# Loading the second quarter of w in eight transfers instead of four, row sets 0 and 1 of all quadrants ahead of row sets 2 and 3

## The chip, the core and the metric

The kernel runs on one core of a Trainium2 chip. The metric is the time of one launch on the device in microseconds (us); for the kernel before, the median of 8 runs is 905.83 us (905.59 to 906.26). A profiled execution gives, besides its time, the span between the first and the last instruction of its trace, and all positions below ("at 14.59") are us from the start of that span.

The core's engines are written as in the profile: PE (matrix multiply), PEld (its weight loads), DVE (vector), ACT (scalar), POOL and SP. POOL and SP also issue transfers; q0 is the queue of those that POOL issues, q1 and q10 those that SP and ACT issue.

## What is computed

```python
B, S, D = 16, 2048, 1024          # x (B,S,D), w (D,D), decay (D), all float32
xw = x @ w
out[:, 0, :] = xw[:, 0, :]
for t in range(1, S):
    out[:, t, :] = decay * out[:, t - 1, :] + xw[:, t, :]
```

A matrix product of 32768 x 1024 by 1024 x 1024, and behind it, for every column of every batch, a first-order recurrence along the 2048 time steps.

## The kernel before

**Tiling.** The 32768 rows of x are cut into 64 chunks of 512 time steps; two chunks make a group. For each group the 1024 output columns are cut into 8 blocks n of 128. One (group, n) is a tile: PE accumulates 128 columns by 1024 steps in PSUM, over K = 8 blocks k of 128 contraction rows, in bf16. Then ACT, POOL and DVE run the recurrence, DVE turns the result back, and SP stores it. There are some 4,000 matmuls of 128x512.

**x.** `load(c, q, j0, j1)` (L101) issues from POOL the transfer of quadrant q (256 of the 1024 contraction rows, on 32 partitions) of chunk c, cast to bf16 on the way. DVE turns it by blocks of 32 (`turn`, L110), and ACT or DVE spreads it into `xt` (`part`, L119). The matmuls of the first chunks read partly `xw` (straight from the turn) and partly `xt`.

**w.** w comes in four quarters (h, e): h is the half of the columns, e the parity of the rows. `stage[h, e]` holds a quarter as it lands; `settle(h, e, m, copy)` (L300) copies row set m (m = 0 to 3) of it into `wsb`, block k = 2m + e. So k = 0, 2, 4, 6 come from e = 0 and k = 1, 3, 5, 7 from e = 1. Quarter (0, 0) is loaded by SP and ACT in float32; the other three by POOL, cast to bf16. `load_w` (L293) issues one transfer for each quadrant of a quarter, in the order 0, 2, 1, 3.

**The order.** All work is emitted in an order written out by hand: `agenda` is a list of deeds, a letter and a number, and the order within one engine's queue is the order of the list. The first line (key -99) is what concerns us, with these letters:

- `M0` to `M3` (`load_half`): the four quadrant transfers of one half of chunk 0 (M0, M1) or chunk 1 (M2, M3), 128 KB each in bf16
- `U0`, `U1`, `U2` (`load_part`, L339): the quarters (0, 1), (1, 0) and (1, 1) of w
- `K0` to `K3`: matmuls that only keep PE busy, each set behind the landing of a quadrant of M0
- `E0` to `E15`: turns of one row set of half a chunk on DVE; `G` and `F`: their spreading on ACT and DVE (E0 to E3 belong to M0, E4 to E7 to M1, E8 to E11 to M2, E12 to E15 to M3)
- `W4 w5 W6 W7`: `settle` of quarter (0, 1), row sets 0 to 3, W on DVE and w on ACT; later `W8` to `W11` settle (1, 0), and `w12` to `w15` settle (1, 1)
- `L`: one more quadrant of a later chunk of x

The transfers of POOL use eight completion semaphores in turn. A transfer therefore waits, on POOL's queue, until the one eight places before it has landed; what stands behind it on that queue waits too.

**Step 0 of PE** is special. In order, for the first four blocks n at once: the even k on chunk 0's two halves (from `xw`, 128x256, 32 matmuls), the odd k on chunk 0 (from `xt`, 128x512, 16 matmuls: k = 1, 3, 5, 7, four each), then chunk 1's first half (k in pairs, 32 matmuls of 128x256), then its second half. So PE needs, in this order: M0 and M1, then row sets 0 to 3 of quarter (0, 1), then M2, then M3. Blocks n = 4 and up need the quarters (1, 0) and (1, 1).

Of the kernel before, what the change touches and what calls it, by code (L numbers as in the profile page):

```python
# [14 lines left out]
def _ap(ap_obj: bass.AP, new_ap, extra_offset=0):  # L15
    return dataclasses.replace(
        ap_obj,
        ap=[list(p) for p in new_ap],
        offset=ap_obj.offset + extra_offset,
    )  # L20
# [5 lines left out]
def kernel(  # L26
# [26 lines left out]
    nc = tc.nc  # L53
    pin = tc.keep_in_program_order
    B, S, D = x.shape
# [3 lines left out]
    P = 32  # L59
    CQ = D // NQ  # L60
    K = CQ // P
    M = K // 2
# [4 lines left out]
    CH = D // 2  # L67
# [12 lines left out]
    def quad(q):  # L80
        return slice(q * P, (q + 1) * P)
# [184 lines left out]
    class Outlet:  # L266
# [7 lines left out]
        def store(self, b, t0):  # L274
# [3 lines left out]
            for i, q in enumerate((0, 2, 1, 3)):  # L278
# [9 lines left out]
    stage = {(0, 0): room[0][:, 0:size],  # L288
             (0, 1): room[0][:, size:size * 3 // 2].bitcast(BF16),
             (1, 0): room[1][:, 0:size // 2].bitcast(BF16),  # L290
             (1, 1): room[1][:, size // 2:size].bitcast(BF16)}

    def load_w(queues, h, e):  # L293
        for i, q in enumerate((0, 2, 1, 3)):
            pin(queues[i % len(queues)].dma_start(  # L295
                out=stage[h, e][quad(q)].rearrange("p (m d) -> p m d", m=M),
                in_=_ap(w, [[2 * D, P], [2 * P * D, M], [1, CH]],
                        (q * CQ + e) * D + h * CH)))

    def settle(h, e, m, copy):  # L300
        src = stage[h, e][:, m * CH:(m + 1) * CH]
# [5 lines left out]
    rows = const.tile([128, 2, P], FP32, name="rows")  # L307
    touch = const.tile([128, 1], BF16, name="touch")
    load_w((nc.sync, nc.scalar), 0, 0)
    pin(nc.vector.memset(idle, 0.0))  # L310
    pin(nc.vector.memset(rows, 0.0))
# [13 lines left out]
    for q in range(NQ):  # L325
        pin(nc.sync.dma_start(
            out=rows[q * P:q * P + R],
            in_=_ap(decay, [[P, R], [CH, 2], [1, P]], q * CR)))
# [8 lines left out]
        spin(3 if q < NQ - 1 else 2, gates[q])  # L337

    def load_part(i):  # L339
        load_w((nc.gpsimd,), *((0, 1), (1, 0), (1, 1))[i])  # L340

    def part_one(i, copy):
        part(i // 8, copy, i % 4, i % 4 + 1, *halves[i // 4 % 2])
# [60 lines left out]
    def turn_and_load(c):  # L404
# [16 lines left out]
        "w": lambda i: settle_one(i, nc.scalar.copy),  # L421
        "M": load_half,
        "U": load_part,
        "E": lambda i: turn(i // 8, *halves[i // 4 % 2], i % 4, i % 4 + 1),
        "F": lambda i: part_one(i, nc.vector.tensor_copy),
# [15 lines left out]
        "L": lambda i: load(*loads.pop(0)) if loads else None,  # L441
    }
    agenda = {
        -99: "M0 M1 U0 M2 M3 U1 U2 w0 W1 w2 W3 K0 K1 K2 K3 E0 E1 G0 E2 G1 E3 F2 G3 E4 E5 G4 E6 G5 E7 F6 G7 W4 w5 W6 W7 D E8 E9 G8 E10 G9 E11 F10 G11 E12 L E13 G12 L E14 G13 E15 L F14 G15",
        0: "p0 z0 W8 W9 W10 W11",
        1: "g0",
        2: "L S1 L",
# [186 lines left out]
```

## Time and profile before

| | us |
|---|---|
| median of 8 runs | 905.83 |
| the profiled execution, its own time | 905.89 |
| its span | 904.1 |
| PE busy | 891.6 (99%) |
| DVE busy | 825.7 (91%) |
| ACT busy | 684.4 (76%) |
| POOL busy | 655.2 (72%) |
| PE idle before L131 matmuls | 5.2, of which 0.7 for `wsb` from DVE |

Busy is the sum of instructions, idle is the time that an engine sat still in front of a group of instructions, and the releaser is what ended it. Issuing a transfer occupies POOL (some 0.55 to 0.65 us each), and the time from issue to landing is listed for itself.

### The profile page before, as it was taken

Reading aid. Unit: us, or ns where it says so; the run is one execution under the profiler, and the core shown is the slowest. Engines: PE = TensorE matmul, PEld = TensorE weight load, DVE = VectorE, ACT = ScalarE, POOL = GpSimd, SP = SyncE. Lnnn points to the kernel's source line nnn. Section 1 sums busy time; section 2 is a strip of 40 time slices with the busy share of each in tenths; the row PEclk is TensorE's granted clock in tenths of the full one; section 3 lists DMA queues with packets and bytes.
Section 4 is the critical chain, followed back from the end, with each engine's and each line's share of the span. In section 5 each row is a group of like instructions: output and inputs, shape, how many; then the busy total and the mean of one; then the engine's idle time right before and its main releaser. Section 6 shows DMA issues by size and latency. Waiting matters only on the chain.

```text
span 904.1 us, 11988 instructions
## 1 busy us (share of the span) xinstructions
PE 891.6 (99%) x4119; PEld 411.0 (45%) x4201; DVE 825.7 (91%) x628; ACT 684.4 (76%) x951; POOL 655.2 (72%) x753
## 2 busy tenths in 40 slices
PE   8999999999999999999999999999999999999997
PEld 5544444444444444444444444444444444444444
DVE  4999998999999999999998999999999999999997
ACT  4889867777877877877778778778777787787742
POOL 7888678777767768777677677787777776776622
PEclk9999999999999999999999999999999999999999
DMA  9999999999999999999999999999999999999868
GB/s 191 197 215 215 231 238 212 215 230 251 242 240 256 250 244 260 248 249 228 225 235 231 221 232 229 228 228 230 228 227 225 234 233 223 227 235 207 175 146 229
DMA packets 402542, 204.77 MB, mean 226 GB/s; under 512 B 8752, under 2 KB 401456, under 8 KB 402480
## 3 DMA queue, kind: packets, MB, share of 16 engines
q1 hardware_dynamic: 265168, 134.76, 61.0%
q0 software_dynamic: 137024, 68.70, 56.7%
q8 instruction: 33, 0.54, 0.2%
q10 hardware_dynamic: 288, 0.52, 0.2%
q14 instruction: 29, 0.24, 0.1%
HBM read 138.42 MB, written 134.22 MB: 302 GB/s over the span
## 4 chain that ended last, share of the span: by engine, by line
PE 95%; DMA 1%; DVE 1%; issue 1%; ACT 1%; POOL 0%; DVEq 0%; POOLq 0%
PE ps L131 94%; PE spare L131 1%; DVE so L221 1%; DMA xb<-in_x_dram 1%; DMA ot<-in_w_dram 1%; ACT xs L183 0%; ACT xt L123 0%; DVE so L201 0%; POOL ot L295 0%; POOL xs L196 0%; ACT h L169 0%; DVE ot L258 0%; PE spare L383 0%; PE ps L383 0%; DVE h L387 0%
## 5 line engine op out<-in xcount | busy, mean ns | idle before, releaser
L131 PE MATMUL ps<-xt,wsb 128*128 128x512 bf16 x3942 | 863.5, 378 | 5.2 <-DVE wsb L302 0.7
L131 PEld LDWEIGHTS <-wsb 128*128 128x128 bf16 x4152 | 405.9, 98 | 480.2 <-DVE wsb L302 1.0
L196 POOL TENSOR_TENSOR xs<-h,xs 128x512 f32<-128x512 f32 (+1 forms) x189 | 241.9, 1280 | 190.0 <-ACT h L169 84.8
L183 ACT COPY xs<-ps 128x1024 f32<-128x1024 f32 (+1 forms) x189 | 188.8, 999 | 154.7 <-PE ps L131 144.3
L258 DVE STREAM_TRANSPOSE ot<-so 128x1024 f32<-128x1024 f32 (+1 forms) x260 | 300.1, 1191 | 2.1 <-POOL so L190 1.1
L246 POOL TENSOR_TENSOR so<-h,xs 128x512 f32<-128x512 f32 (+1 forms) x189 | 240.5, 1274 | 44.9 <-ACT h L169 28.2
L123 ACT COPY xt<-xw 128x2048 bf16<-128x2048 bf16 (+1 forms) x136 | 242.3, 1790 | 7.3 <-DVE xw L115 7.1
L105 POOL DMA_DIRECT2D xb<-in_x_dram x264 | 174.0, 660 | 3.0 <-DMA ot<-in_w_dram 1.2
L169 ACT ACTIVATE h<-so,dec 128x512 f32<-128x512 f32 (+1 forms) x189 | 144.9, 767 | 28.6 <-DVE so L201 25.5
L115 DVE STREAM_TRANSPOSE xw<-xb 128x2048 f32<-128x2048 f32 (+1 forms) x78 | 147.3, 1901 | 7.1 <-DMA xb<-in_x_dram 7.1
L201 DVE TENSOR_TENSOR_SCAN so<-spare,keep,xs 128x512 f32<-128x512 f32 (+1 forms) x96 | 119.3, 1244 | 26.6 <-POOL xs L196 26.2
L201 DVE TENSOR_TENSOR_SCAN so<-spare,xs 128x512 f32<-128x512 f32 x93 | 113.2, 1219 | 27.4 <-POOL xs L196 24.6
L169 ACT ACTIVATE h<-ps,dec 128x512 f32<-128x512 f32 (+1 forms) x189 | 129.7, 686 | 0.0
L221 DVE TENSOR_TENSOR_SCAN so<-dec,ps 128x1024 f32<-128x1024 f32 x34 | 76.9, 2261 | 1.3 <-ACT h L169 1.0
L221 DVE TENSOR_TENSOR_SCAN so<-dec,keep,ps 128x1024 f32<-128x1024 f32 (+1 forms) x36 | 77.2, 2145 | 0.5 <-PE ps L131 0.3
L250 ACT COPY keep<-so 128x1 f32<-128x1 f32 x136 | 25.3, 189 | 12.9 <-DVE so L221 12.6
L192 ACT COPY so<-keep 128x1 f32<-128x1 f32 x96 | 18.3, 191 | 2.0 <-DVE ot L258 1.8
L131 PE MATMUL ps<-xw,wsb 128*128 128x256 bf16 (+1 forms) x68 | 11.2, 301 | 0.0
L190 POOL MEMSET so<- 128x1 f32 x93 | 10.7, 117 | 0.3 <-DVE ot L258 0.3
L131 PE MATMUL spare<-xt,wsb 128*128 128x512 bf16 (+1 forms) x48 | 10.0, 335 | 0.0
L295 POOL DMA_DIRECT2D ot<-in_w_dram x12 | 6.5, 544 | 3.0 <-DMA xb<-in_x_dram 2.1
L320 PE MATMUL spare<-idle 128*128 128x512 bf16 x22 | 6.3, 452 | 1.2 <-DVE idle L310 1.2
(37 smaller groups left out, 36.3 us busy)
## 6 DMA issues: line engine op xcount, KB each, us to landing
out_dram<-ot SPq DMA_DIRECT2D x248, 512.0 KB, 10.9
xb<-in_x_dram POOLq DMA_DIRECT2D x248, 256.0 KB, 7.8
out_dram<-ot SPq DMA_DIRECT2D x12, 256.0 KB, 4.8
xb<-in_x_dram POOLq DMA_DIRECT2D x16, 128.0 KB, 5.8
ot<-in_w_dram POOLq DMA_DIRECT2D x12, 128.0 KB, 5.1
out_dram<-xb SPq DMA_DIRECT2D x3, 256.0 KB
ot<-in_w_dram ACTq DMA_DIRECT2D x2, 256.0 KB, 5.0
ot<-in_w_dram SPq DMA_DIRECT2D x2, 256.0 KB, 4.6
```

Of the source, the lines that this page charges most:

```text
L105: pin(nc.gpsimd.dma_start(out=xb_of[c][quad(q), j0:j1], in_=_ap(x, [[D, P], [P * D, j1 - j0], [1, CQ]], (b * S + t0 + j0 * P) * D + q * CQ)))
L115: pin(nc.vector.transpose(out=dst.rearrange("p (m j i) -> p j m i", m=M, i=P)[:, j0:j1, m0:m1], in_=src.rearrange("p (j m c) -> p j m c", ...
L123: pin(copy(out=xt_of[c][:, m0:m1, :, j0 * P:j1 * P], in_=src))
L131: pin(nc.tensor.matmul(out=ps[:, t0:t1] if ps.shape[1] >= t1 else ps, lhsT=lhs, rhs=rhs, start=(k == 0 and t0 == start), stop=(k == K - 1),))
L169: pin(nc.scalar.activation(out=h, in_=src, func=mybir.ActivationFunctionType.Copy, scale=dec[:, self.n:self.n + 1]))
L183: pin(nc.scalar.copy(out=self.xs, in_=self.ps))
L196: pin(nc.gpsimd.tensor_tensor(out=odds, in0=self.g, in1=odds, op=ALU.add))
L201: pin(nc.vector.tensor_tensor_scan(out=so[:, 3:T + 2:2], data0=squares[-1][:, n:n + 1].to_broadcast([128, T // 2]), data1=self.xs[:, 1:T:2 ...
L221: pin(nc.vector.tensor_tensor_scan(out=so[:, t + 2:t + 2 + size], data0=dec[:, n:n + 1].to_broadcast([128, size]), data1=ps, initial=befor ...
L246: pin(nc.gpsimd.tensor_tensor(out=self.so[:, 2:T + 2:2], in0=self.h, in1=self.xs[:, 0:T:2], op=ALU.add))
L250: pin(nc.scalar.copy(out=self.keep, in_=self.so[:, self.T + 1:self.T + 2]))
L258: pin(nc.vector.transpose(out=outlet.ot[:, :, c0:c0 + P], in_=self.so[:, 2 + t0:2 + t0 + nj * P].rearrange("p (i t) -> p i t", t=P)))
```

## The change

`load_w` takes two further arguments, the first and last row set that it loads, and quarter (0, 1) is loaded by two calls: row sets 0 and 1 of the four quadrants, then row sets 2 and 3. Each transfer has 64 rows of 512 elements in place of 128. The list gains one deed, the later ones are renumbered, and all the rest is as it was.

```diff
-    def load_w(queues, h, e):
+    def load_w(queues, h, e, m0=0, m1=M):
         for i, q in enumerate((0, 2, 1, 3)):
             pin(queues[i % len(queues)].dma_start(
-                out=stage[h, e][quad(q)].rearrange("p (m d) -> p m d", m=M),
-                in_=_ap(w, [[2 * D, P], [2 * P * D, M], [1, CH]],
-                        (q * CQ + e) * D + h * CH)))
+                out=stage[h, e][quad(q)].rearrange("p (m d) -> p m d", m=M)[:, m0:m1],
+                in_=_ap(w, [[2 * D, P], [2 * P * D, m1 - m0], [1, CH]],
+                        (q * CQ + e + m0 * 2 * P) * D + h * CH)))
...
     def load_part(i):
-        load_w((nc.gpsimd,), *((0, 1), (1, 0), (1, 1))[i])
+        load_w((nc.gpsimd,), *((0, 1, 0, 2), (0, 1, 2, M), (1, 0), (1, 1))[i])
...
-        -99: "M0 M1 U0 M2 M3 U1 U2 w0 W1 w2 W3 K0 K1 K2 K3 ...
+        -99: "M0 M1 U0 U1 M2 M3 U2 U3 w0 W1 w2 W3 K0 K1 K2 K3 ...
```

On POOL's queue the order becomes: eight transfers of chunk 0 (M0, M1), eight of quarter (0, 1) (64 KB each in bf16), eight of chunk 1 (M2, M3), eight of the quarters (1, 0) and (1, 1), and then chunk 2. POOL issues 4 transfers more. On DVE, `W4` waits for the first four transfers of the quarter alone, and `W6` for the other four; on ACT, `w5` needs the first four. The order of instructions on PE, DVE, ACT and SP is unchanged.

## The prediction

> **What bounds the kernel now.** First the page: PE is busy for 99% of the span, and the chain that ended last runs on it.
>
> ```profile
> span 904.1 us, 11988 instructions
> PE 891.6 (99%) x4119; PEld 411.0 (45%) x4201; DVE 825.7 (91%) x628; ACT 684.4 (76%) x951; POOL 655.2 (72%) x753
> ```
>
> So a delay of PE near the start, with PE hardly ever idle behind it, arrives at the end in full. Next, what PE waited for between 8 and 60 us:
>
> ```profile
> PE spare L320 <- ACT gate L336: 0.9, 1, 0.9
> PE ps L131 <- DVE wsb L302: 0.7, 1, 0.7
> ```
>
> The second wait (us in total, times, longest) is the only one that this change can remove. The timeline shows it, on PE and on DVE (start, duration, in brackets the idle time before):
>
> ```profile
> 14.31 0.27 PE L131 MATMUL spare<-xw,wsb 128*128 128x256 bf16 x1
> 15.29 0.82 PE L131 MATMUL ps<-xt,wsb 128*128 128x512 bf16 x2 [0.70 <-DVE wsb L302]
> ```
> ```profile
> 14.94 0.70 DVE L302 COPY wsb<-ot 128x512 bf16<-128x512 bf16 x3 [1.09 <-DMA ot<-in_w_dram]
> 17.66 1.43 DVE L115 STREAM_TRANSPOSE xw<-xb 128x256 f32<-128x256 f32 x4 [1.47 <-DMA xb<-in_x_dram]
> 20.38 0.77 DVE L115 STREAM_TRANSPOSE xw<-xb 128x256 f32<-128x256 f32 x2 [0.98 <-DMA xb<-in_x_dram]
> ```
>
> W4 starts when the four transfers of quarter (0, 1) have landed (the last at 9.74 + 5.07 = 14.81, by the chain in order of time), and PE sits still until 15.29. But the next two things on DVE, the turns of M2 (17.66) and M3 (20.38), wait for transfers as well. So I read the queue that feeds all of them, POOL's:
>
> ```profile
> 7.89 0.55 POOL L295 DMA_DIRECT2D ot<-in_w_dram  x1 [1.85 <-DMA xb<-in_x_dram]
> 8.68 1.61 POOL L295 DMA_DIRECT2D ot<-in_w_dram  x3 [0.23 <-DMA xb<-in_x_dram]
> 10.40 3.04 POOL L105 DMA_DIRECT2D xb<-in_x_dram  x5
> 13.78 1.99 POOL L105 DMA_DIRECT2D xb<-in_x_dram  x3 [0.34 <-DMA ot<-in_w_dram]
> ```
>
> The reader is to see that POOL issues no faster than landings allow: the ninth transfer goes out at 7.89, 0.29 after the first landed (1.32 + 6.28 = 7.60). Eight are in flight, and a quarter of w holds four of the eight places. Finally the rate, from 10.6 to 13.3 us:
>
> ```profile
> DMA packets 711, 0.54 MB, mean 198 GB/s; under 512 B 66, under 2 KB 711, under 8 KB 711
> ```
>
> One 128 KB transfer takes 131072 / 198 = 0.66 us of the DMA engines. Single issues, asked for one by one, landed 5.1 (M2's first, issued at 10.40) to 5.4 us after issue. Is the rest of these 5 us queueing, which shorter transfers would shorten, or fixed? A stretch in which q0 was empty tells:
>
> ```profile
> q1 hardware_dynamic: 2004, 1.01, 102.9%
> xb<-in_x_dram POOLq DMA_DIRECT2D x2, 256.0 KB, 10.3
> ```
>
> From 129.0 to 132.7 only SP's stores move; POOL's issue at 130.15 shows its first packet at 132.74, so 2.6 us from issue to first byte. At the start, an engine that had run dry took w's first packet at 10.66, 2.8 us after the issue at 7.89. I take 2.7. Before the change M2's first transfer is issued at 10.40 and ready at 13.1, while w's packets last until 13.6 to 14.0: the queue keeps busy with only half a microsecond to spare.
>
> **The change, part by part.**
>
> *The lanes and POOL.* The first eight issues after M1 leave when M0's and M1's transfers land: 7.89, 8.67, 9.2, 9.7 (POOL's own 0.54 each), 10.40, 10.92, 11.62, 12.26. The last four are the times at which M2 goes out now; w's second half takes them. M2 follows POOL-bound, 0.58 each after 12.26 + 0.54: at 12.8, 13.4, 13.9 and 14.5, in place of 10.40 to 12.27. All later transfers shift too.
>
> *What the wait at 14.59 becomes.* The first half's last transfer, issued at 9.7, lands at 9.7 + 2.7 + 0.33 (64 KB) + 0.8 (w's last packets to its landing: 14.0 to 14.81) = 13.5 in place of 14.81. DVE is free at 13.84, so W4 is done by 14.2; ACT's w5 is done by 14.9, needed at 15.45. The 0.70 goes. But W6 needs the second half: 12.26 + 2.7 + 0.33 + 0.8 = 16.1, and 0.48 more to the matmul (15.29 - 14.81) is 16.57, against 14.59 + 1.73 (half of the 3.46 us of the odd k, 15.29 to 18.75) = 16.32. A new stall of about 0.25. PE reaches chunk 1 at 18.3, 0.45 earlier.
>
> *What is late next: M2.* Its first packet comes at 12.8 + 2.7 = 15.5. The eight halves of w, 0.33 us each and issued 0.5 to 0.8 apart, can't keep the engines busy until then. Four transfers of 0.66 end at 18.1, and with 0.8 they have landed at 18.95 in place of 17.53. From landing to PE: 0.13 (17.66 - 17.53), one turn of 0.40, 0.08 to the matmul, 0.61. PE starts chunk 1 at 19.55 in place of 18.75, a stall of 1.25 that is nowhere now. Bounds: if the shorter queue frees nothing, the last issue takes 5.3 us as today, 14.5 + 5.3 + 0.6 = 20.4, 1.65 later than now; if the first byte came after the issue's own 0.54 us, M2 would land as today (17.53), and PE would start at 18.13, 0.6 earlier. I stay near the 2.7, the row nearest to it.
>
> The Trainium skill says otherwise ("DMA: Bandwidth & Descriptors", section "Latency and other measured facts"): about 1 us to the first byte of a transfer issued by GpSimd; this case's packets show 2.6 to 2.8. By the page M2 would be ready at 13.8, just in time, and the sum would be a gain of about 0.6. The same page, section "Bandwidth", advises batching and calls transfers under 64 KB descriptor-dominated, which speaks against the change; the trace has no 64 KB transfer to test it.
>
> *M3, w's other quarters, chunk 2.* All follow 1.4 to 1.9 late. M3 would be turned from about 21.9 in place of 20.38, and PE needs its first row set at 19.55 + 3.56 (18.75 to 22.31) = 23.1: hidden. W8 to W11 start near 24.5 in place of 22.98, needed from 26.7: hidden. The quarter (1, 1) lands at 25.8 now, and ACT settles it from 26.69, so 0.9 of slack, to which PE's own 0.8 is added (ACT's work ahead of it waits for PE); it lands at 27.3 to 27.7 against 27.5. Here 0 to 0.3 more may be lost, as PEld already waits 0.8 in all for these copies; I take 0.1. Chunk 2's last quadrant lands at 31.5 now and DVE turns it at 33.52: hidden, as is chunk 3 (turned until 40.24, read from 43.17). Were that cover gone, each could cost up to 1 us.
>
> *Sum:* -0.70 + 0.25 + 1.25 + 0.1 = +0.9 us. The profiled execution took 905.89, 0.06 above the median of the runs; the span of 904.1 becomes about 905.0, with the same 1.8 around it: 906.8 us.
>
> **The rivals.**
>
> A. *Landings no quicker than now* (slower for good): each transfer keeps its 5.1 to 5.4 us however little is queued, so that PE waits for M2 until 20.4, and ACT for the quarter (1, 1), +0.1 to +0.4 more. It decides once M2 lands later than 18.14 + 1.8 = 19.9 or so, where the loss passes 0.2%. For it: the eight issues from 10.40 to 15.09 all show this latency. Against it: 0.66 us steps between landings show that it holds queueing. +1.65 + 0.35 = +2.0: 907.9 us.
>
> B. *M2 is not late* (faster): the queue holds enough to bridge, and the 0.70 is gained up to the point where M2 is awaited, 0.6. For it: now the engines never ran dry. Against it: the 2.6 to 2.8 us to the first byte. 905.3 us.
>
> C. *No net effect*: the halves cover part of the hole, M2 lands at 18.1, PE starts chunk 1 as now, 905.8 us. For it: M2's slack of 0.6 today. Against it: M2's issues, bound by POOL, are 2.2 us later.
>
> D. *The clock*: two pauses of PE within four microseconds lower its granted clock. Against it: it stays at 1.00 through today's 0.9 and 0.7. At half the clock for 3 us, 1.5 on top of 0.9: 908.3 us.
>
> **How the numbers follow.** Forecast 0.54, A 0.25, B 0.11, C 0.07, D 0.03. A measurement of this kernel tells about 0.2%, 1.8 us, from no change. The forecast, from +0.4 to +1.5, lies within it, as do B and C, and a small part of A lies below 1.8 us; most of A and D are beyond. Faster by over 0.2% would need a gain that no row offers: 0.02. Within 0.2%: 0.72. Slower: 0.26. The range leaves out B's and A's outer halves: 905.4 to 908.2; the time is the forecast's, 906.8.
>
> **What would show it.** Right: W4 starts at about 13.9, and PE goes from the even to the odd k without the 0.7; M2's first issue at 12.8; a dip of the DMA rate between 11.5 and 15.5; a PE wait for xw of about 1.2 us ending near 19.5, and the span's end about 0.9 later. Wrong: no wait for M2's turn (B, C), M2's landings 5 us or more after issue (A), a granted clock below 1.00 behind 16 us (D), or PE waits of other names later.

## The result and the profile after

| us | before | after |
|---|---|---|
| median beside each other | 905.97 (905.25 to 906.67, 31 runs) | 908.35 (907.44 to 909.55, 11 runs) |
| profiled execution, its span | 905.89, 904.1 | 907.73, 905.9 |

The ratio is 1.0028 (95% interval 1.0021 to 1.0036): 2.4 us slower, a little beyond the 0.2% that this kernel's measurement can tell, and 0.15 above the range. The profiled execution shows 1.8 of the 2.4; the runs of the changed kernel lie further apart than those before (2.1 against 1.4 us), and no profile shows where the other 0.6 goes. The mean granted clock that is on record for every execution says something of it: the three slowest of the eleven (909.22 to 909.55) have 0.997, those with 0.999 or more lie between 907.44 and 908.75, and no execution of the kernel before that was run beside the experiments has less than 0.998. In the run i2_pause_idle below, one stretch of 3.4 us at half clock, which costs PE 1.7 us, leaves a mean of 0.997. So the clock probably fell once in some executions of the changed kernel; the profiled one is not among them, so this isn't shown.

The page, and then PE's waits from 8 to 60 us (total, times, longest):

```profile
span 905.9 us, 11994 instructions
PE 893.1 (99%) x4119; PEld 411.0 (45%) x4201; DVE 825.8 (91%) x628; ACT 684.0 (76%) x951; POOL 657.2 (73%) x757
```
```profile
PE ps L131 <- DVE xw L115: 1.6, 1, 1.6
PE ps L131 <- ACT h L169: 0.3, 1, 0.3
```

The wait for `wsb` is gone, a longer one for M2's turn stands in its place, and there is a new one for ACT. (The 0.7 that is gone was large for this kernel: in the profiles of e4, e5 and g1, whose code is the same up to there, PE waits 0.2 for `wsb`.) Where they lie, by PE's timeline and DVE's:

```profile
14.53 0.81 PE L131 MATMUL ps<-xt,wsb 128*128 128x512 bf16 x2
...
19.79 0.84 PE L131 MATMUL ps<-xw,wsb 128*128 128x256 bf16 x6 [1.64 <-DVE xw L115]
...
23.44 2.27 PE L131 MATMUL ps<-xw,wsb 128*128 128x256 bf16 x16
...
43.83 1.89 PE L131 MATMUL ps<-xt,wsb 128*128 128x512 bf16 x8 [0.28 <-ACT h L169]
```
```profile
13.87 0.32 DVE L302 COPY wsb<-ot 128x512 bf16<-128x512 bf16 x1
15.26 0.49 DVE L302 COPY wsb<-ot 128x512 bf16<-128x512 bf16 x2 [1.06 <-DMA ot<-in_w_dram]
...
19.29 1.42 DVE L115 STREAM_TRANSPOSE xw<-xb 128x256 f32<-128x256 f32 x4 [2.98 <-DMA xb<-in_x_dram]
...
22.94 1.43 DVE L115 STREAM_TRANSPOSE xw<-xb 128x256 f32<-128x256 f32 x4 [1.91 <-DMA xb<-in_x_dram]
...
26.08 1.03 DVE L302 COPY wsb<-ot 128x512 bf16<-128x512 bf16 x4 [1.41 <-DMA ot<-in_w_dram]
27.03 2.27 DVE L221 TENSOR_TENSOR_SCAN so<-dec,ps 128x1024 f32<-128x1024 f32 x1
```

W4 runs at 13.87 without a wait, W6 at 15.26. M2's turn is at 19.29 (before 17.66), M3's at 22.94 (20.38), W8 to W11 at 26.08 (22.98). From 26 on DVE has no pause in which to make up its 2.7 us. The 2.27 us for 16 matmuls at 23.44 (2.0 before) is PE paced by the turns of M3. The last quarter of w, on ACT's timeline (before: 26.69, without a wait):

```profile
28.62 2.18 ACT L302 COPY wsb<-ot 128x512 bf16<-128x512 bf16 x4 [0.40 <-DMA ot<-in_w_dram]
```

The wait for ACT at 43.83 comes by way of POOL. POOL has two jobs in one queue, issuing transfers and its part of the recurrence (L196 and L246). Held up by late landings, it begins the issues of chunk 2 at 23.73 (before 21.17) and reaches L246 2.6 late; ACT, which waits for POOL before its next copy, is 2.6 late from there on and frees the PSUM buffer late. (DVE is as late; the run g1_scan_first below helps to tell the two apart.) Before, then after, on POOL and on ACT:

```profile
33.15 2.54 POOL L246 TENSOR_TENSOR so<-h,xs 128x512 f32<-128x512 f32 x2
34.48 1.01 ACT L183 COPY xs<-ps 128x1024 f32<-128x1024 f32 x1 [1.12 <-POOL so L246]
```
```profile
35.75 2.54 POOL L246 TENSOR_TENSOR so<-h,xs 128x512 f32<-128x512 f32 x2
37.09 1.01 ACT L183 COPY xs<-ps 128x1024 f32<-128x1024 f32 x1 [1.02 <-POOL so L246]
```

The cause of the lateness, on POOL's timeline and in the windows (stretch, then busy time of PE, PEld, DVE, ACT, POOL, the granted clock, the DMA share, GB/s). M2 is issued from 12.90, eight transfers without a pause:

```profile
10.69 2.23 POOL L295 DMA_DIRECT2D ot<-in_w_dram  x4 [0.21 <-issue]
12.90 4.70 POOL L105 DMA_DIRECT2D xb<-in_x_dram  x8
```
```profile
13.00:14.00 1.00, 1.00 (x11) 0.84 (x10) 1.00 (x4) 1.00 (x3) 1.00 (x2) 1.00 0.83 123
14.00:15.00 1.00, 0.95 (x9) 0.68 (x8) 0.19 (x1) 0.88 (x2) 1.00 (x3) 1.00 0.56 63
15.00:17.00 2.00, 2.00 (x10) 0.94 (x10) 0.99 (x5) 0.00 (x0) 2.00 (x4) 1.00 1.24 159
17.00:19.00 2.00, 1.15 (x6) 0.40 (x5) 0.00 (x0) 0.00 (x0) 1.95 (x5) 1.00 1.33 155
19.00:21.00 2.00, 1.21 (x11) 1.02 (x11) 1.71 (x5) 1.23 (x3) 1.54 (x4) 1.00 1.20 145
21.00:23.00 2.00, 2.00 (x20) 1.75 (x19) 0.09 (x2) 0.43 (x1) 0.89 (x2) 1.00 1.25 179
```

Before the change the same stretches show 187, 187, 192, 192, 203 and 203 GB/s; two of these windows:

```profile
15.00:17.00 2.00, 1.66 (x7) 0.80 (x9) 1.12 (x6) 0.53 (x1) 1.78 (x4) 1.00 1.44 192
17.00:19.00 2.00, 2.00 (x12) 1.00 (x11) 1.34 (x4) 0.86 (x2) 1.57 (x3) 1.00 1.44 192
```

So there is a hole at 14, which was expected, and then 145 to 159 GB/s for six microseconds more, which was not. The granted clock stays at 1.00 in this execution.

PE's start after the change minus before, at the same matmuls:

| place | PE later by (us) | step to it | forecast of the step |
|---|---|---|---|
| first matmuls of chunk 0 | +0.15 | | |
| odd k of chunk 0 | -0.75 | -0.90 | -0.70 |
| chunk 1 (M2) | +1.04 | +1.79 | +0.25 + 1.25 |
| its second half's end (M3) | +1.43 | +0.39 | 0 |
| odd k of n = 4 (`w12` to `w15`) | +1.94 | +0.51 | +0.1 |
| near 43 (PSUM buffer freed late) | +2.38 | +0.44 | 0 |
| PE's last matmul | +2.05 | -0.33 | 0 |

The -0.33 is one step at 872 us, where PE waits for DVE before the change and not after it. Another 0.2 goes behind the last matmul: the span is 1.8 longer.

### The profile page after: what moved, and what is told of

Its sections match the earlier page's. It is cut to its first block, busy times and chain, and to the rows that moved or that the text cites. A ratio compares the mean times of both kernels' runs of the same rounds, so it can differ in the third digit from the quotient of the medians.

```text
span 905.9 us, 11994 instructions
## 1 busy us (share of the span) xinstructions
PE 893.1 (99%) x4119; PEld 411.0 (45%) x4201; DVE 825.8 (91%) x628; ACT 684.0 (76%) x951; POOL 657.2 (73%) x757
## 4 chain that ended last, share of the span: by engine, by line
PE 94%; POOL 2%; DMA 1%; issue 1%; ACT 1%; DVE 0%; POOLq 0%
PE ps L131 93%; POOL xb L105 1%; DMA ot<-in_w_dram 1%; DMA xb<-in_x_dram 1%; PE spare L131 1%; POOL ot L295 1%; POOL xs L196 0%; ACT xt L123 0%; ACT xs L183 0%; POOL so L246 0%; PE spare L383 0%; ACT h L169 0%; PE ps L383 0%; DVE h L387 0%; POOL so L190 0%
## 5 line engine op out<-in xcount | busy, mean ns | idle before, releaser
L196 POOL TENSOR_TENSOR xs<-h,xs 128x512 f32<-128x512 f32 (+1 forms) x189 | 242.0, 1281 | 190.5 <-ACT h L169 89.7
L246 POOL TENSOR_TENSOR so<-h,xs 128x512 f32<-128x512 f32 (+1 forms) x189 | 240.3, 1273 | 43.3 <-ACT h L169 27.9
L295 POOL DMA_DIRECT2D ot<-in_w_dram x16 | 8.6, 537 | 4.4 <-DMA xb<-in_x_dram 3.3
```

The costliest lines, as they stand in the source:

```text
L196: pin(nc.gpsimd.tensor_tensor(out=odds, in0=self.g, in1=odds, op=ALU.add))
L246: pin(nc.gpsimd.tensor_tensor(out=self.so[:, 2:T + 2:2], in0=self.h, in1=self.xs[:, 0:T:2], op=ALU.add))
```

## The experiments

The theory at the outset: four more issues on POOL make M2 late, and the empty queue is what costs. The kernel before was run beside each on the same chip; its medians there were 905.60 (the runs whose names begin with e), 905.78 (f and g), 905.70 (h) and 905.81 (i).

### Is it the order, or the number of transfers?

**e2_by_quadrant**: the changed kernel's eight transfers, both halves of a quadrant next to each other.

```diff
-        load_w((nc.gpsimd,), *((0, 1, 0, 2), (0, 1, 2, M), (1, 0), (1, 1))[i])
+        if i == 0:
+            for q in (0, 2, 1, 3):
+                for m0 in (0, 2):
+                    load_w((nc.gpsimd,), 0, 1, m0, m0 + 2, (q,))
```

> Eight transfers of 64 KB as in the changed kernel, but quadrant after quadrant, both halves of one together, so that W4 has to wait for the seventh of the eight. Theory (what is gained at the odd k is lost again in front of M2): W4 starts near 15 and PE waits 1 us for wsb, but PE starts chunk 1 at 19.8 as in the changed kernel, and the time is the same, 908.3 us. Rival (the early row sets keep 0.9 us of gain in the changed kernel): 909.2 us.

Measured: 908.21, ratio 1.0030 (1.0021 to 1.0040): the time that the theory gave, and the same as the changed kernel's. Its parts were not as forecast: PE waits 0.15 for `wsb`, not 1, and starts chunk 1 at 20.42, not 19.8. The early row sets are worth a start of the odd k at 14.53 instead of 14.88, and PE then waits 1.9 instead of 1.6 for M2's turn.

**f1_six**: quadrants 0 and 2 whole, 1 and 3 in halves, six transfers.

```diff
+        load_w((nc.gpsimd,), *((0, 1, 0, M, (0, 2)), (0, 1, 0, 2, (1, 3)),
+                               (0, 1, 2, M, (1, 3)), (1, 0), (1, 1))[i])
```

> Quarter (0, 1) in six transfers: quadrants 0 and 2 whole, then row sets 0 and 1 of quadrants 1 and 3, then their row sets 2 and 3. M2 goes out at about 11.6, and with the 1.3 to 1.8 us from issue to first packet that the runs with a hole showed it is ready at about 13.3, while w's packets last until 13.4. Theory (the cost begins where the queue runs dry): no dip of the rate, M2 is turned at 17.7 as before, W4 starts near 14, and 0.4 to 0.6 us are gained: 905.3 us. Rival (each further transfer costs its share, 2.4 us for four): 907.0 us.

Measured: 906.86, 1.0011 (1.0003 to 1.0020). The theory's gain failed; the rival's number held. M2 was issued from 11.68, early enough, and the rate fell all the same: 161, 159, 148 and 158 GB/s in the four stretches of 2 us from 13 on. PE waited 1.1 for M2.

**f2_sixteen**: one row set in each transfer, 32 KB, sixteen of them.

```diff
+        load_w((nc.gpsimd,), *((0, 1, 0, 1), (0, 1, 1, 2), (0, 1, 2, 3), (0, 1, 3, M),
+                               (1, 0), (1, 1))[i])
```

> Quarter (0, 1) in sixteen transfers of 32 KB, row set after row set. Theory: POOL issues M2 only at 17.1, the rate falls below 100 GB/s for some 5 us, M2 is turned near 22.5 and PE starts chunk 1 near 23, 4.2 us later than before; with the later quarters' share 911 us. Rival (the cost of the changed kernel is the one hole of its size and does not grow with the number): 908.3 us.

Measured: 912.76, 1.0077 (1.0064 to 1.0091). The theory's direction held, its size did not: 1.8 more than it expected. PE starts chunk 1 at 23.98 (expected near 23), and the windows show what comes on top (the third number from the right is the granted clock):

```profile
20.00:22.00 2.00, 0.17 (x1) 0.00 (x0) 0.00 (x0) 0.00 (x0) 2.00 (x4) 1.00 1.15 126
22.00:24.00 2.00, 0.02 (x1) 0.02 (x1) 0.52 (x2) 0.04 (x1) 1.51 (x4) 0.66 1.28 160
24.00:26.00 2.00, 2.00 (x10) 1.38 (x10) 1.21 (x4) 1.62 (x3) 1.50 (x4) 0.50 1.29 172
```

PE waits 3.8 us for M2, the granted clock falls to 0.50, and the next 5.5 us of matmuls (23.98 to some 29.5) take twice their time: 2.7 us.

**f3_half_left_out**: the first four transfers alone; row sets 0 and 1 are used in place of 2 and 3.

```diff
-        src = stage[h, e][:, m * CH:(m + 1) * CH]
+        c = m % 2 if (h, e) == (0, 1) else m
+        src = stage[h, e][:, c * CH:(c + 1) * CH]
...
-        -99: "M0 M1 U0 U1 M2 M3 ...
+        -99: "M0 M1 U0 M2 M3 ...
```

> Row sets 2 and 3 of quarter (0, 1) are not loaded, and row sets 0 and 1 are used in their place: as many transfers as before the change, 256 KB less, and row sets 0 and 1 as early as in the changed kernel. Theory (the early row sets are worth up to 0.9 us at the odd k if M2 follows in time): W4 near 13.9, no wait of PE for wsb nor for xw, 905.0 us. Rival (transfers of 64 KB by themselves, four of the eight in flight, make the queue run dry): M2 late again, over 906.5 us.

Measured: 905.81, 0.9999 (0.9990 to 1.0008). Neither held. The odd k start early and M2 is not late (PE waits 0.2), with no issue more than before and 256 KB less to move, yet the rate falls, from 13 on:

```profile
13.00:15.00 2.00, 2.00 (x18) 1.59 (x18) 2.00 (x8) 2.00 (x4) 2.00 (x5) 1.00 1.26 157
15.00:17.00 2.00, 2.00 (x11) 0.92 (x10) 0.56 (x3) 0.07 (x1) 2.00 (x4) 1.00 1.28 161
17.00:19.00 2.00, 2.00 (x15) 1.19 (x13) 1.73 (x5) 1.49 (x3) 0.82 (x3) 1.00 1.05 127
```

M3 lands at 20.61 (before 20.25), and the gain is gone again by 41 us. Even a second quarter of half the size, in early row sets, brings nothing.

### Is an empty queue enough by itself?

**e5_hole**: the kernel before, with four memsets on POOL ahead of M2, so that only M2's issue is late.

```diff
+    def pause(i):
+        for _ in range(4):
+            pin(nc.gpsimd.memset(scrap, 0.0))
...
+        "O": pause,
-        -99: "M0 M1 U0 M2 M3 ...
+        -99: "M0 M1 U0 O0 M2 M3 ...
```

> The kernel before, with quarter (0, 1) in its four transfers of 128 KB, and four memsets (some 2 us) on POOL ahead of M2's issue. Theory (a hole in the queue is the cost, whoever makes it): M2 is turned near 19.3, the DMA rate stays at 150 to 170 GB/s for some microseconds behind the hole, M3 and the later quarters are 2.5 us late, about 908.3 us. Rival (the small transfers disturb the rate, not the hole): the rate returns to 190 GB/s at once, M3 and the quarters are only 1.6 us late, about 907.0 us.

Measured: 908.27, 1.0028 (1.0018 to 1.0039), the theory's 908.3. With w's transfers as they were, a late M2 (issued from 12.72) gives the changed kernel's time, and its rates behind the hole. Not all of the theory came: M2 is turned at 18.65, not 19.3, and M3 lands only 1.65 later than before, as the rival had it; the quarters (1, 0) and (1, 1) land 2.7 and 2.1 later. The rates:

```profile
13.00:15.00 2.00, 1.78 (x17) 1.29 (x15) 1.55 (x6) 1.82 (x4) 2.00 (x4) 1.00 0.88 118
15.00:17.00 2.00, 1.95 (x9) 0.92 (x11) 0.82 (x5) 0.17 (x1) 2.00 (x5) 1.00 1.25 145
17.00:19.00 2.00, 1.56 (x8) 0.59 (x6) 0.35 (x1) 0.00 (x0) 2.00 (x5) 1.00 1.29 163
19.00:21.00 2.00, 1.85 (x17) 1.57 (x17) 1.38 (x5) 1.66 (x3) 1.16 (x3) 1.00 1.32 160
```

### Are w's later quarters hidden, as the prediction had it?

**e4_late_quarters**: the kernel before, with four unused transfers of 64 KB behind M3, so that nothing is late but the quarters (1, 0) and (1, 1) and what follows them.

```diff
+    def extra(i):
+        for q in (0, 2, 1, 3):
+            pin(nc.gpsimd.dma_start(
+                out=scrap[quad(q)],
+                in_=_ap(w, [[2 * D, P], [2 * P * D, 2], [1, CH]], q * CQ * D)))
...
-        -99: "M0 M1 U0 M2 M3 U1 U2 ...
+        -99: "M0 M1 U0 M2 M3 O0 U1 U2 ...
```

> The kernel before with four more transfers of 64 KB (their data is not used) behind M3 and ahead of the quarters (1, 0) and (1, 1), so that only these quarters and what follows are late, by 1.3 to 2.5 us. Theory (W8 to W11 hold up the scans behind them on DVE, and w12 to w15 hold up PE): PE as before until 25.9, then 0.4 to 0.6 later at w12 to w15 and as much again near 41 when ACT frees a PSUM buffer late, 906.9 us. Rival (the prediction: the lateness is hidden but for 0.1): 906.0 us.

Measured: 907.35, 1.0017 (1.0008 to 1.0026), 1.75 us slower than the kernel before, so "hidden" is refuted. (1, 0) lands 2.1 and (1, 1) 1.7 us later than before, and its two timelines show where PE pays:

```profile
28.31 3.89 PE L131 MATMUL ps<-xt,wsb 128*128 128x512 bf16 x16 [0.86 <-ACT wsb L302]
```
```profile
27.64 2.18 ACT L302 COPY wsb<-ot 128x512 bf16<-128x512 bf16 x4 [1.17 <-DMA ot<-in_w_dram]
```

ACT stands still for 1.17 in front of `w12`, PE for 0.9 behind it. Near 41 PE loses 0.5 more to a PSUM buffer that ACT frees late. The theory put this down to DVE, which is 1.8 us late from its first scan on; the next run tests that.

**g1_scan_first**: the same, but DVE takes the scan `S1` ahead of W8 to W11, so that late weights do not hold up the recurrence.

```diff
-        0: "p0 z0 W8 W9 W10 W11",
+        0: "p0 z0",
...
-        2: "L S1 L",
+        2: "L S1 W8 W9 W10 W11 L",
```

> As e4_late_quarters, but on DVE the scan of tile 1 stands ahead of W8 to W11. Theory (these four copies, waiting for the late quarter (1, 0), hold up DVE, which has no idle time between 25 and 60 us, and ACT and PSUM behind it): the scan starts at 24.3 in place of 26.2, the step of 0.5 us that PE loses near 41 goes, PE's step at w12 to w15 stays: 906.9 us, 0.4 less than e4_late_quarters. Rival (DVE's delay is not what PE loses near 41): 907.3 us or more, as PE now waits for W8.

Measured: 907.54 (906.78 to 910.13), 1.0022 (1.0013 to 1.0031); the rival held. PE now waits 1.0 for W8 to W11 where it waited for `w12`, and the step near 41 shrinks only from 0.49 to 0.37. That the order on DVE is what makes the late quarters dear is not confirmed. The traces point to POOL instead. On DVE the turn of a later chunk starts at 34.07, in e4 at 35.34, so DVE is 1.3 ahead there. But POOL stands where it stood (before: 33.15), and ACT waits for it, 2.04 in place of 0.84. First e4, then g1:

```profile
34.71 2.53 POOL L246 TENSOR_TENSOR so<-h,xs 128x512 f32<-128x512 f32 x2
36.02 1.01 ACT L183 COPY xs<-ps 128x1024 f32<-128x1024 f32 x1 [0.84 <-POOL so L246]
```
```profile
34.62 2.55 POOL L246 TENSOR_TENSOR so<-h,xs 128x512 f32<-128x512 f32 x2
35.95 1.01 ACT L183 COPY xs<-ps 128x1024 f32<-128x1024 f32 x1 [2.04 <-POOL so L246]
```

POOL is 1.5 late in both. No run has taken POOL's part of the recurrence out from behind its issues, so this is read from the waits, not tested.

### Four transfers over all quadrants

**e1_row_sets**: one transfer for each row set, over all four quadrants, 128 KB each, so that nothing is issued more often than before.

```diff
+    def load_set(h, e, m):
+        pin(nc.gpsimd.dma_start(
+            out=stage[h, e][:, m * CH:(m + 1) * CH],
+            in_=_ap(w, [[CQ * D, NQ], [2 * D, P], [1, CH]],
+                    (e + m * 2 * P) * D + h * CH)))
```

> Quarter (0, 1) in four transfers of 128 KB, each one row set of all quadrants: the order of the change, but as many transfers and bytes as before. Theory (the four more places in the queue are what costs, the early row sets are a gain): no dip of the DMA rate, W4 starts near 13.9, PE's wait of 0.7 for wsb is gone, the turn of M2 starts at 17.7 as before, and PE gains what M2 leaves, about 0.6 us: 905.4 us. Rival (loading by row sets across quadrants is what costs): as the changed kernel, 908.3 us.

Measured: 907.24, 1.0023 (1.0013 to 1.0033). Neither. M2 was issued early (10.33 to 12.76), but the row sets themselves moved slowly, and only then did the rate return at once to 192 and 196:

```profile
13.00:15.00 2.00, 2.00 (x20) 1.54 (x18) 1.62 (x6) 1.73 (x4) 0.45 (x2) 1.00 1.21 127
15.00:17.00 2.00, 1.95 (x10) 0.93 (x11) 0.66 (x3) 0.55 (x1) 1.64 (x4) 1.00 1.31 173
17.00:19.00 2.00, 1.60 (x8) 0.61 (x7) 0.48 (x3) 0.00 (x0) 1.68 (x4) 1.00 1.44 192
```

The first and the last of the 16 landing signals of one such transfer lie 1.8 to 2.6 us apart, against 0.9 to 1.2 for the same quarter in the kernel before. The Trainium skill ("DMA: Bandwidth & Descriptors", "Why a DMA increments its semaphore by 16 and not by 1") says that the slowest dimensions of both sides set over how many engines a transfer is spread: the largest number up to 16 that divides both, here 128 and 4, so 4. The wider spread fits that; the trace doesn't name the engines.

### Why does the rate stay low behind the hole?

Two thoughts: too little is in flight, since POOL brings 128 KB at a time into an empty queue; or the queue is slow for a while whatever is in it. **h2_before_whole** and **h1_after_whole** load chunk 1 in four transfers of 256 KB, in the kernel before and in the changed one.

```diff
-            load(i // 2, q, *halves[i % 2])
+            if i < 2:
+                load(i // 2, q, *halves[i % 2])
+            elif i == 2:
+                load(1, q)
```

> The kernel before with chunk 1 of x loaded by four transfers of 256 KB in place of eight of 128 KB. Both theories: no stretch in which little moves, since chunk 1 is issued from 10.40 as before; the rate stays at 185 or more from 12 to 21, chunk 1 has landed near 20.2 (where its last transfer lands now), PE starts it near 20.8 (+2.1), and the time is 907.8. If the rate falls below 175 here as well, larger transfers are slower in themselves, and the other run tells nothing about bytes in flight.

> The changed kernel with chunk 1 of x loaded by four transfers of 256 KB, a whole quadrant each, in place of eight of 128 KB (same bytes, four issues fewer, and all turns of chunk 1 wait for the whole). In the changed kernel the rate stays at 130 to 173 GB/s from 16 to 21 us, behind the stretch at 14 us in which little moves. Theory (bytes in flight): the rate is low since POOL brings new work only 128 KB at a time into an empty queue; with 256 KB an issue 1 MB is in flight by 15, and the rate is back at 185 or more from 15.5 to 21; chunk 1 has landed at 14.6 + 5.3 + 0.8 = 20.7, PE starts it near 21.3 (+2.5 against before), w's other quarters follow at 23.3 and 25.9 as before, and the time is 908.3. Rival (the queue is slow for some 6 us behind a stretch in which it ran dry, whatever is in flight): 130 to 173 GB/s from 15.5 to 21 again; chunk 1 has landed at 22.1 or later, PE starts it at 22.7 (+3.9), 909.5 or more.

Measured: h2 908.66, 1.0032 (1.0021 to 1.0043), with 142 GB/s in one microsecond (15 to 16) and 177 or more from 16 to 26. The condition on record, below 175, was met for that microsecond, so larger transfers are slow in themselves at most briefly. PE starts chunk 1 at 21.82 (expected 20.8), and of the eight executions the four slowest (908.93 to 909.76) have a mean clock of 0.997, the other four 0.999. h1 913.06, 1.0078 (1.0063 to 1.0093). Its windows:

```profile
14.00:16.00 2.00, 1.95 (x13) 1.03 (x11) 0.19 (x1) 0.76 (x2) 2.00 (x5) 1.00 0.89 92
16.00:18.00 2.00, 1.69 (x9) 0.69 (x8) 1.01 (x5) 0.00 (x0) 1.74 (x4) 1.00 0.89 96
18.00:20.00 2.00, 0.51 (x3) 0.11 (x2) 0.00 (x0) 0.00 (x0) 0.29 (x1) 1.00 1.38 185
```

With all of chunk 1, 1 MB, issued by 15.3, the rate is lower still, 96 GB/s. "Too little in flight" falls. The rival's PE start (22.7 or later) held at 23.40. But the rate came back at 18, when POOL had stopped issuing (POOL busy 0.29 in place of 1.74): a third thought, that issuing slows the transfers. **i1_pause_busy** puts six memsets, **i2_pause_idle** a wait for chunk 1's third quadrant, between chunk 1 and the next quarter:

```diff
     def load_part(i):
+        if i == 2:
+            for _ in range(6):
+                pin(nc.gpsimd.memset(pause, 0.0))
```
```diff
+        if i == 2:
+            pin(nc.gpsimd.tensor_copy(out=pause[quad(2), 0:1], in_=xb_of[1][quad(2), 0, 0:1]))
```

> The changed kernel with chunk 1 in four transfers of 256 KB, as before, and six memsets of 128x512 float32 on POOL (0.61 us each by the earlier run with four) between chunk 1's last issue (15.3) and the next quarter of w: POOL is busy but issues nothing from 15.3 to 19. Without them the rate was 140, 113 and 78 GB/s from 15 to 18, while POOL issued without a break, and 178 to 201 from 18, when it had stopped. Theory (while POOL issues, transfers that it is hardly ahead of run slowly): 185 GB/s or more from 16 to 19; chunk 1 has landed near 20.6, PE starts it at 21.3 in place of 23.4, and since that pause of PE is some 2.8 us, about 909 (without the halved clock, 910 with it). Rival (the queue is slow for 3 us or more behind a stretch in which it ran dry, whatever POOL does): again 80 to 140 GB/s from 15 to 18, PE starts chunk 1 near 23.4, and the time is 913 or more.

> The same with one POOL copy of 32 elements of chunk 1's third quadrant in place of the six memsets: POOL stands idle from 15.3 until that quadrant has landed. Theory (issuing slows the transfers): as with the memsets, 185 GB/s or more from 16 until POOL issues again near 19.3; PE starts chunk 1 near 21.3; about 909 to 910. If the memsets' run stays slow and this one is quick, it is POOL's work of any kind; if both stay at 80 to 140 GB/s from 15 to 18, it is the queue itself (rival), and the time is 913 or more.

Measured: 912.30, 1.0072 (1.0055 to 1.0089), and 912.67, 1.0077 (1.0062 to 1.0092); PE starts chunk 1 at 23.50 and 23.43. The third thought falls too; the rival's rates and start held, its time (913 or more) is missed by 0.7 and 0.3. The windows of i1, then of i2:

```profile
16.00:18.00 2.00, 2.00 (x11) 0.90 (x10) 1.17 (x4) 0.00 (x0) 1.83 (x4) 1.00 0.92 117
18.00:20.00 2.00, 0.45 (x3) 0.10 (x1) 0.00 (x0) 0.00 (x0) 1.94 (x5) 1.00 1.40 188
...
26.00:28.00 2.00, 2.00 (x14) 1.47 (x12) 1.48 (x6) 0.78 (x2) 1.67 (x4) 0.62 1.28 192
```
```profile
16.00:18.00 2.00, 2.00 (x10) 0.88 (x9) 0.63 (x4) 0.00 (x0) 0.00 (x0) 1.00 0.65 68
18.00:20.00 2.00, 0.11 (x1) 0.00 (x0) 0.00 (x0) 0.00 (x0) 0.00 (x0) 1.00 1.37 184
...
22.00:24.00 2.00, 0.57 (x3) 0.39 (x3) 1.07 (x4) 0.59 (x2) 2.00 (x4) 0.86 0.42 60
24.00:26.00 2.00, 2.00 (x12) 1.34 (x10) 2.00 (x8) 2.00 (x5) 2.00 (x5) 0.50 0.99 148
26.00:28.00 2.00, 2.00 (x16) 1.61 (x15) 0.30 (x1) 0.71 (x2) 1.70 (x3) 0.79 0.91 137
```

In i2, with POOL entirely idle from 16 to 18, the rate is 68 GB/s. And i2 ran its queue dry a second time, at 22 to 23, and was slow a second time: 148, 137 and 151 GB/s from 24 to 30, where i1, which did not run dry there, moved the same transfers at 202, 192 and 193. So in all seven runs in which POOL's queue ran dry or nearly so (the changed kernel, e2, e5, f2, h1, i1, i2) it was slow for 3 us or more afterwards, with 128 or 256 KB a transfer, with POOL issuing, busy or idle.

"Slow" is not even. In half microseconds h1 moves 186 and 179 GB/s from 15.5 to 16.5, and then 47 and 41 until 17.5; i1 147 and 189, then 105 and 52; i2 188 and 143, then 22 and 22. So about one transfer of 256 KB moves at the full rate, and a second hole follows, though the three other transfers had been issued by 15.4. Why these come so late is not shown. In the changed kernel, with 128 KB a transfer, there is no second hole: 126 to 185 in every half microsecond from 15 to 21. Nor is it the work of DVE and ACT at that moment: both stand still from 17 to 19 in the changed kernel, where the rate is 155.

What the DMA engines wait for in that time is open: single packets of 150 to 860 ns appear in the changed kernel there, up to 1.3 us in h1, against 60 ns for x's packets (98 for w's) in the steady stretch, and nothing in the trace says why. An empty queue is enough (e5), but it isn't needed: f1 and f3, whose queue held less but never emptied, dipped too, and so did e4 and g1, to 155 to 175 and 121 to 180 GB/s from 25 to 31 us, after the four transfers of 64 KB.

## Why the prediction was wrong, by its steps

- **What bounds it** was right: of the 2.38 by which PE is late at 45 us, all but 0.33 is there at its last matmul, and 1.8 at the end of the span.
- **The lanes and POOL** were right: M2's issues forecast at 12.8 to 14.5, found at 12.90 to 14.66.
- **The 0.70 goes**: right, and even the new stall of 0.25 at W6 did not come; the second half landed at 15.14, not at 16.1. The last two halves took 2.74 and 2.76 from issue to landing, where the sum had 3.8. But the 0.70 is one execution's; 0.2 in three others says that the change had less to win than the sum took.
- **M2 late**: right in the event, 19.79 against 19.55, and rival B's condition failed. But that it is so near is luck, as two errors cancelled: the first packet came 1.7 us after the issue (14.58 - 12.90), not 2.7, and four transfers then moved at 146 to 172 GB/s (windows of 1 us from 15 to 19), which is 0.76 to 0.90 each, not 0.66. Of the two rows behind the 2.7, the one at 7.89 had M1's transfers ahead of it, which landed until 11.99, so it held queueing. The page's 1 us to a first byte (named in the prediction) is nearer than the 2.7 taken from the two rows: 1.3 in e5, 1.7 here. It would still have led astray, since the rate behind it is what fell.
- **The step that failed: "M3, w's other quarters, chunk 2. All follow 1.4 to 1.9 late ... hidden ... I take 0.1."** It took for granted that the queue is back at 198 GB/s once it has work. It was at 145 to 159 until 21: M3 landed 2.6 later, (1, 0) 3.1, (1, 1) 2.7. And the cover was thinner than read: M3 cost 0.39 and (1, 1) on ACT 0.51. POOL's own part of the recurrence stands behind its issues on the same queue, and the prediction counted nothing for it: it came 2.6 late and, as the waits of ACT and g1 have it, cost 0.44 near 43 us. That is 1.34 in place of 0.1. With the 0.24 by which chunk 1 was later than forecast (+1.04 against +0.80) and the 0.33 given back, PE's end is 1.15 later than forecast (2.05 against 0.9). e4 shows the second half of the error without the first: late quarters, and what comes behind them on POOL, cost 1.75 us alone.
- **Rival A** (907.9) ended near, by another road: M2 landed 4.2 to 4.5 us after issue, not 5.1 to 5.4, and M3 and the quarters 4.6 to 7.0. **D** (908.3) ended nearest in number. In the profiled execution it did not come: the clock held through the 1.64. In others it probably did, by their mean clock of 0.997, and the forecast gave it 0.03; how much of the 0.6 that the profile doesn't show is due to it stays open.

No version tried beats the kernel before; of those that leave nothing out, f1_six, at +1.1, comes nearest.

## What to carry to other kernels

A transfer queue that is just full enough is a resource: before splitting transfers, count how far the issuing engine is ahead, and price not only the hole but several microseconds of a lower rate behind it, for every transfer there. "Hidden" has to be shown for each engine that the late data passes through, and for the engine that issues the transfers: POOL, held up by late landings, did its part of the recurrence 2.6 us late, and PE paid for it some 8 us later. And a short wait that is seen in the profile may be the price of a full queue behind it; it may also be much shorter in the next execution (0.7 here, 0.2 in three others).

## What the runs showed of the hardware that was not expected

- POOL's queue, once dry, moves 68 to 163 GB/s (in windows of 2 us) for 3 to 6 us in place of 190 to 200, with up to 1 MB waiting in it (h1, i1, i2, e5, after); with 256 KB a transfer, this is a second hole behind some 256 KB at the full rate.
- The granted clock falls to 0.50 in a long pause of PE: in the profiles, pauses of 3.8 (f2), 4.9 (h1), 5.1 (i1) and 5.3 us (i2) did it, 1.6 to 2.5 us (after, e2, h2) did not. The mean clock of 0.997 in four of h2's eight executions and in three of the changed kernel's eleven suggests that shorter pauses do it at times; no profile shows one. The stretch at 0.50 lasted 6.8 us in f2, h1 and i1 and 3.4 us in i2, and ended 3.4 to 5.7 us after PE had resumed. The Trainium skill ("TensorE: Matmul & The Clock Gate", "What's actually happening") has this gate, at half or full rate and with about 3.4 us of sustained work to open it; the runs fit the half rate, and took 3.4 to 5.7 us.
